# Joining an out projection and a feed-forward by halves of the tokens

## The chip, the cores and the metric

The kernel runs on one core of a Trainium2 chip. The metric is the device time of one execution in microseconds (us), the median of repeated runs. A core has five engines that each work through a list of instructions of their own, in order: TensorE (PE, the matrix engine), VectorE (DVE), ScalarE (ACT), GpSimd (POOL) and SyncE (SP, which here starts the loads). They wait for one another by semaphores.

## The reference, cut to what matters

The program computes two blocks of a transformer, one after the other, for 512 tokens of width 1024, all in fp32. The change lies in the opening block, between its mixer and its feed-forward:

```python
mixed = groups @ w_out[i]                       # out projection, 1024 x 1024
h = h + rmsnorm(mixed, ln_post_mix[i])          # first norm
f = rmsnorm(h, ln_pre_ffn[i])                   # second norm
g, up = jnp.split(f @ w_gate_up[i], 2, axis=-1) # 1024 x 5632
y = (jax.nn.silu(g) * up) @ w_down[i]           # 2816 x 1024
h = h + rmsnorm(y, ln_post_ffn[i])
```

The second block needs, among much else, a vector `mod = cond @ ada_w[i] + ada_b[i]` per layer, with `ada_w` of 1024 x 6144. This product of a single row is done on DVE, beside the matmuls of other stages.

## The kernel before, in words

Values lie with features on the 128 partitions and the 512 tokens in the free dimension. A tensor of width 1024 is eight tiles 128x512 (`X0..X7`, and `M0..M7` in buffers named `hh0..hh7`). A fp32 matmul is made of three faster ones: each operand is split into a high part, rounded to a shorter form, and a low part, the rest; `mm3` issues low weight x high value, high x high, high x low. Weights come in slabs: one load of 128x1024 (`raw`, four buffers), then in `unit` per half a cast on ACT (`whi`) and a subtraction on DVE (`wlo`), seven buffers of 512 columns each. A slab of w_gate_up is 24 matmuls and gives 128 features for all tokens; a slab of w_out is 12 here (its other half was done earlier), one of w_down 66.

A norm has several steps (`norm_cols`, `norm_rows`): squares on ACT, their sum over eight tiles on POOL or DVE (`acc`), four matmuls of one column against ones (PE, `tt<-ones1k,acc`), plus epsilon on DVE (`ms`), power -1/2 on POOL (`rc`), four small matmuls that spread the result over the partitions (`tt<-ident,rc`), a copy on DVE. The scale of the second norm is applied not to the operand but to the outputs of gate_up (`g` and `u` times `R`), so its matmuls can start before it is known.

The join goes in this order. For each of eight w_out slabs DVE multiplies the result with the scale of the attention half and adds it to M (L550, L551), ACT squares it, POOL adds the square to `macc` (DVE for the last), and ACT scales M by its column of ln_post_mix (L554, L555). Then the first norm; then `post` (L630, L631) for each of eight tiles, M x R and X + M, and `split_scaled`: ACT scales X into a high part (L275), DVE computes the low part (L276). The first four gate_up slabs run together, tile by tile of X (three `mm` banks and `po`), so that PE can begin with the first tile of X. Then come the second norm and gate_up slabs 4 to 43, one by one. A pair of slabs gives g and u of one of 22 feature tiles: DVE multiplies both with R (L733, L736), ACT applies Silu, POOL multiplies (L737), ACT and DVE split the result into `Hh` and `Hl` (L266, L267). w_down reads all 22.

From slab 4 on each slab is followed by `self.step()`, one step of the ada chain: a load of 128x1024 into the only `ada` buffer and one multiply-and-reduce on DVE (a dot, L813). The next load can start only when the dot before it is done. 40 dots belong to the first group of columns.

The order of instructions on each engine is made by a scheduler from the data flow and the order of the code; `self.order(True)` pins PE's list to the order of the code, up to `self.order(False)`. `keep_in_program_order` keeps the dots in sequence. `homes` opens two pools of memory, at the bottom and the top, and puts the tile names of a list into the lower one.

## Time and profile before

| what | value |
| --- | --- |
| three runs, median (lowest to highest) | 1908.2 us (1907.35 to 1908.96) |
| the profiled execution, and its span | 1911.36 us, 1909.7 us |
| PE busy | 1871.8 us, 98% of the span |
| DVE, ACT, POOL busy | 68%, 47%, 20% |
| chain of waits that ended last | PE 79%, DVE 5%, ACT 1% |
| single waits of PE above 1.1 us | 7.3 (start of the program), 6.2, 5.4, 3.5, 2.0, 1.7, 1.4, 1.2, 1.2 |
| mean granted clock of PE | 0.992 of full speed |

The waits of 5.4, 3.5, 1.7, 1.4 and one of the two of 1.2 us belong to the stretch that the change touches, from 205 to 250 us. In a row of a timeline stand the start and the duration in us, the engine, the line, the operation, the tiles written and read, the shape, the number of instructions put together, and in brackets how long the engine was idle before it and what ended that. Matmuls overlap, so their duration is longer than their distance from start to start.

### The profile page before, as it was taken

The page shows a single profiled execution, that of the slowest core. Times are in us where ns is not written, and L with a number is a line of the kernel's source. Part 1 is how long each engine was busy: PE and PEld are TensorE (multiplying, and loading weights), DVE is VectorE, ACT ScalarE, POOL GpSimd, SP SyncE. Part 2 cuts the span into 40 slices and gives each one's busy share as a digit, 9 for nine tenths or more (in the row PEclk, how much of TensorE's full clock was granted, in tenths as well). Part 3 has the DMA queues.
Part 4 walks back from the last instruction along what each step waited for, and adds up shares of the span by engine and source line. Part 5 has one row for each costly group of instructions (what it writes and reads, how often), then busy time and mean ns, then how long its engine had stood idle before and what let it go on. Part 6 is the DMA issues. An engine that isn't in the chain of part 4 may idle for free.

```text
span 1909.7 us, 24071 instructions
## 1 busy us (share of the span) xinstructions
PE 1871.8 (98%) x8610; PEld 1505.3 (79%) x8610; DVE 1289.6 (68%) x2354; ACT 897.2 (47%) x1664; POOL 373.4 (20%) x348
## 2 busy tenths in 40 slices
PE   8999799999999999999999999999899999999999
PEld 6887688888887887777888888887666788888887
DVE  8686876566346767885988774578977677666431
ACT  5465532323334455554644443345489755444321
POOL 3201421111000303332111110013454311111000
PEclk9999899999999999999999999999999999999999
DMA  5232155556464232322465555622222133222331
GB/s 207 89 91 78 53 186 183 184 183 187 158 214 144 98 121 81 86 67 69 133 206 194 195 173 169 208 97 100 83 67 68 31 106 115 96 96 94 97 116 44
DMA packets 70381, 236.93 MB, mean 124 GB/s; under 512 B 8085, under 2 KB 8677, under 8 KB 70262
## 3 DMA queue, kind: packets, MB, share of 16 engines
q1 hardware_dynamic: 69556, 234.47, 37.9%
...
q0 software_dynamic: 128, 0.08, 0.0%
HBM read 226.87 MB, written 2.21 MB: 120 GB/s over the span
## 4 chain that ended last, share of the span: by engine, by line
PE 79%; DVE 5%; issue 1%; ACT 1%; POOL 0%; POOLq 0%; ACTq 0%; DVEq 0%
PE mm L95 47%; PE sc L95 26%; PE po L95 3%; PE tt L98 2%; PE tt L95 1%; DVE isc L1141 1%; DVE m L1140 1%; DVE hl L899 0%; DVE v L1078 0%; DVE rst L223 0%; DVE isc L1121 0%; DVE q L897 0%; ACT A L671 0%; DVE acc L986 0%; DVE rst L224 0%
## 5 line engine op out<-in xcount | busy, mean ns | idle before, releaser
L112 ACT CAST whi<-raw 128x512 fp32r<-128x512 f32 (+1 forms) x550 | 326.7, 607 | 394.7 <-PE mm L95 232.2
L113 DVE TENSOR_TENSOR wlo<-raw,whi 128x512 fp32r<-128x512 f32 (+1 forms) x518 | 379.5, 741 | 193.8 <-ACT whi L112 191.3
L95 PE MATMUL mm<-hh,wlo 128*128 128x512 f32 (+1 forms) x984 | 399.6, 406 | 3.5 <-ACT hh L275 3.5
L95 PE MATMUL mm<-hl,whi 128*128 128x512 f32 (+1 forms) x1016 | 394.9, 392 | 0.0
L95 PE MATMUL mm<-hh,whi 128*128 128x512 f32 (+1 forms) x984 | 385.3, 392 | 0.0
L95 PEld LDWEIGHTS mm<-hl,whi 128*128 128x128 f32 (+1 forms) x1016 | 191.4, 188 | 41.3
L813 DVE CUSTOM_DVE_ANT_0 ada<-ada,bc 128x1024 f32<-128x1024 f32 x112 | 140.3, 1252 | 123.8 <-DMA ada<-in_ada_w 103.7
L95 PEld LDWEIGHTS mm<-hh,wlo 128*128 128x128 f32 (+1 forms) x984 | 185.7, 189 | 47.3 <-issue 8.5
L95 PEld LDWEIGHTS mm<-hh,whi 128*128 128x128 f32 (+1 forms) x984 | 185.8, 189 | 36.2 <-issue 1.1
L95 PE MATMUL sc<-hh,wlo 128*128 128x512 f32 x432 | 168.8, 391 | 0.0
L95 PE MATMUL sc<-hh,whi 128*128 128x512 f32 x432 | 168.4, 390 | 0.0
L95 PE MATMUL sc<-hl,whi 128*128 128x512 f32 x432 | 168.3, 390 | 0.0
L204 POOL TENSOR_TENSOR acc<-acc,sq 128x512 f32<-128x512 f32 x53 | 89.4, 1687 | 395.5 <-ACT sq L209 387.9
L1052 POOL TENSOR_TENSOR g<-g,u 128x512 f32<-128x512 f32 x44 | 63.0, 1432 | 413.0 <-DVE u L1048 358.1
L95 PE MATMUL mm<-Hh,wlo 128*128 128x512 f32 x364 | 143.3, 394 | 0.0
L95 PE MATMUL mm<-Hh,whi 128*128 128x512 f32 x364 | 143.0, 393 | 0.0
L95 PE MATMUL mm<-Hl,whi 128*128 128x512 f32 x364 | 143.0, 393 | 0.0
L266 ACT CAST Hh<-g 128x512 fp32r<-128x512 f32 x66 | 41.0, 622 | 168.4 <-POOL g L737 104.1
L95 PEld LDWEIGHTS sc<-hh,whi 128*128 128x128 f32 x432 | 81.4, 188 | 16.9
L95 PEld LDWEIGHTS sc<-hh,wlo 128*128 128x128 f32 x432 | 81.4, 188 | 16.9
L95 PEld LDWEIGHTS sc<-hl,whi 128*128 128x128 f32 x432 | 81.3, 188 | 16.9
L95 PE MATMUL sc<-Hh,wlo 128*128 128x512 f32 x220 | 86.7, 394 | 0.0
...
## 6 DMA issues: line engine op xcount, KB each, us to landing
...
```

Source lines behind the costliest of these rows:

```text
L95: self.queue(self.nc.tensor.matmul(*args, **kw))
L98: self.queue(self.nc.tensor.transpose(*args))
L112: nc.scalar.copy(hi[:, :w], raw[:, c:c + w])
L113: (eng or nc.vector).tensor_sub(lo[:, :w], raw[:, c:c + w], hi[:, :w].bitcast(F32))
L204: (eng or self.nc.gpsimd).tensor_add(acc, acc, self.square(src))
L266: self.nc.scalar.copy(hi, src)
L813: nc.vector.tensor_tensor_reduce(raw, raw, row, scale=1.0, scalar=0.0, op0=ALU.mult, op1=ALU.add, accum_out=out))
L1052: nc.gpsimd.tensor_mul(g, g, u)
L1140: nc.vector.max(m8, work[qb][:, :L])
L1141: nc.vector.match_replace(work[qb][:, :L], m8, work[qb][:, :L], SENT)
```

## The change

- Slabs 0 to 3 of w_out stay as they were; slabs 4 to 7 are done first for tokens 0 to 255 and then for tokens 256 to 511, with four banks open. All sums of squares for the first norm go to DVE. Squares of the last slab are not added but taken as a second group of column matmuls.
- The columns of the first norm for the first half come after slab 5 of the second half, its rows after slab 6 of the second half; columns of the second half after tile 1 and rows after tile 3 of the feed-forward's first half.
- The first three gate_up slabs (not four) run tile by tile, first for one half of the tokens and then for the other. Slab 3 follows whole, then the columns of the second norm, slab 4, its rows, slab 5. PE's list is pinned until there.
- The column scale of ln_post_mix is part of the first DVE operation of the new `operand`; eight multiplications on ACT go. Its result is scaled by the norm's rows where they lie, without a copy.
- The operand has its own tiles (high parts in the `hl` buffers, low parts in `Hh0..Hl3`), the first four feed-forward tiles lie in `hh` buffers, and the lower pool has `Hh0..Hh12` and `Hl0..Hl12`.
- The first ada step stands in the code behind slab 5; it stood behind slab 4.

```diff
+            def merge(n, ps, hs):
+                m = self.t(at, [P, S], F32, "sb", bufs=2)[:, hs]
+                nc.vector.tensor_mul(m, ps[:, hs], Ra[:, hs])
+                nc.vector.tensor_add(M[n][:, hs], M[n][:, hs], m)
+
+            for n in range(4):
                 if n < 3:
                     ps = pss[n]
                 else:
                     ps = self.mm_ps()
                     self.slabs([ps], [self.unit(a["w_out"][n][:, :512], (512,))], ms[:4])
-                m = self.t(at, [P, S], F32, "sb", bufs=2)
-                nc.vector.tensor_mul(m, ps, Ra)
-                nc.vector.tensor_add(M[n], M[n], m)
-                macc = self.add_square(macc, M[n], eng=nc.vector if n == 7 else None)
-                if n:
-                    nc.scalar.mul(M[n - 1], M[n - 1], self.col("ln_post_mix", n - 1))
-            nc.scalar.mul(M[7], M[7], self.col("ln_post_mix", 7))
-        _, R = self.stats(macc, self.ones1k, out="bc")
-        return X, M, R
+                merge(n, ps, slice(0, S))
+                macc = self.add_square(macc, M[n], eng=nc.vector)
+            last = [self.t(self.sp, [P, S], F32, "sq", bufs=2) for _ in range(2)]
+            pss = [self.mm_ps(), self.mm_ps(), self.sc_ps(), self.sc_ps()]
+            ws = [self.unit(a["w_out"][n][:, :512], (512,)) for n in range(4, 8)]
+            for h in range(2):
+                hs = self.half(h)
+                for n in range(4, 8):
+                    self.slabs([pss[n - 4][:, hs]], [ws[n - 4]], [(hi[:, hs], lo[:, hs]) for hi, lo in ms[:4]])
+                    merge(n, pss[n - 4], hs)
+                    sq = self.square(M[n][:, hs], last[n % 2][:, hs])
+                    if n < 7:
+                        nc.vector.tensor_add(macc[:, hs], macc[:, hs], sq)
+                    if h and n == 5:
+                        tt = self.t(self.pp, [P, 2, S], F32, "tt", bufs=1)
+                        rc = self.half_cols(tt[:, 0, :], macc, last[1], 0)
+                    if h and n == 6:
+                        R = self.half_rows(tt[:, 1, :], rc, 0)
+        return X, M, R, macc, last[1]
+
+
...
+    def half_cols(self, pc, acc, sq, h):
+        nc = self.nc
+        for tb in (2 * h, 2 * h + 1):
+            ts = slice(tb * P, (tb + 1) * P)
+            self.matmul(pc[:, tb:tb + 1], acc[:, ts], self.ones1k[:, 0:1], start=True, stop=False)
+            self.matmul(pc[:, tb:tb + 1], sq[:, ts], self.ones1k[:, 0:1], start=False, stop=True)
+        ms = self.t(self.sp, [P, NB], F32, "ms", bufs=2)[:, :2]
+        nc.vector.tensor_scalar(ms, pc[:, 2 * h:2 * h + 2], EPS, None, op0=ALU.add)
+        rc = self.t(self.sp, [P, NB], F32, "rc", bufs=3)[:, :2]
+        nc.gpsimd.tensor_tensor(rc, ms, self.mhalf[:, :2], op=ALU.pow)
+        return rc
+
+    def half_rows(self, pb, rc, h):
+        for i in range(2):
+            tb = 2 * h + i
+            self.matmul(pb[:, tb * P:(tb + 1) * P], rc[:, i:i + 1].to_broadcast([P, P]), self.ident, start=True, stop=True)
+        return pb
...
-            ps = self.four()
-            w = self.units([a["w_gate_up"][i] for i in range(4)])
+        with self.homes("ffn", [f"H{p}{i}" for p in "hl" for i in range(13)]) as fp:
+
+            xs = [(self.t(self.xp, [P, S], F32R, f"hl{k}", bufs=1), self.t(fp, [P, S], F32R, f"H{'hl'[k % 2]}{k // 2}", bufs=1))
+                  for k in range(KD)]
+
+            def operand(R, hs):
+                for k in range(KD):
+                    (hi, lo), col = xs[k], self.col("ln_pre_ffn", k)
+                    nc.vector.scalar_tensor_tensor(M[k][:, hs], M[k][:, hs], self.col("ln_post_mix", k), R[:, hs], op0=ALU.mult, op1=ALU.mult)
+                    nc.vector.tensor_add(X[k][:, hs], X[k][:, hs], M[k][:, hs])
+                    nc.scalar.activation(hi[:, hs], X[k][:, hs], AF.Copy, scale=col)
+                    nc.vector.scalar_tensor_tensor(lo[:, hs], X[k][:, hs], col, hi[:, hs].bitcast(F32), op0=ALU.mult, op1=ALU.subtract)
+                return [(hi[:, hs], lo[:, hs]) for hi, lo in xs]
+
+            ps = [self.mm_ps() for _ in range(3)]
+            w = self.units([a["w_gate_up"][i] for i in range(3)])
+            for h in range(2):
+                hs = self.half(h)
+                xh = operand(R, hs)
+                for k in range(KD):
+                    self.slabs([p[:, hs] for p in ps], w, xh, ks=[k])
+                    if h == 0 and k == 1:
+                        rc = self.half_cols(self.sc_ps(), macc, last, 1)
+                    if h == 0 and k == 3:
+                        R = self.half_rows(self.sc_ps(), rc, 1)
             for k in range(KD):
-                self.post(X, M, R, k)
-                xs.append(self.split_scaled(X[k], self.col("ln_pre_ffn", k), k))
-            self.slabs(ps, w, xs)
-            for k in range(KD):
-                acc = self.add_square(acc, X[k])
-            _, R = self.stats(acc, self.ones1k)
+                acc = self.add_square(acc, X[k], eng=nc.vector)
+
+            def slab(i, p):
+                self.slabs([p], [self.unit(a["w_gate_up"][i])], xs)
+                ps.append(p)
+
+            slab(3, self.bank("po"))
+            rc = self.norm_cols(acc, self.ones1k)
+            slab(4, self.sc_ps())
+            R = self.norm_rows(rc)
+            slab(5, self.sc_ps())
+            self.order(False)
             self.ada = (step for l in range(2) for step in self.ada_steps(l))
-            hs = []
+            self.turn, hs = 4, []
             for n in range(KF):
                 if n > 1:
                     for j in range(2):
-                        ps.append(self.any_ps())
-                        self.slabs(ps[-1:], [self.unit(a["w_gate_up"][2 * n + j])], xs)
+                        if n > 2:
+                            slab(2 * n + j, self.any_ps())
                         self.step()
...
+                if n < 4:
+                    hi, lo = (self.t(self.xp, [P, S], F32R, f"hh{2 * n + j}", bufs=1) for j in range(2))
+                    nc.scalar.copy(hi, g)
+                    nc.vector.tensor_sub(lo, g, hi.bitcast(F32))
+                    hs.append((hi, lo))
+                else:
+                    hs.append(self.split(g, n, "H", fp))
```

The lists of instructions move as follows. PE before, at the end of w_out: the last three matmuls (`mm_2204`), columns and rows of the first norm, and the first matmuls of gate_up slabs 0 to 2 (`mm_2257` to `mm_2259`).

```order
L95 MATMUL mm_2204<-hl_549_2001,wlo_2208 128x512
L95 MATMUL mm_2204<-hl_549_2001,whi_2207 128x512
L95 MATMUL mm_2204<-hl_550_2002,whi_2207 128x512
L95 MATMUL tt_2235<-ones1k_101,acc_2084 128x1 [waits DVE_49,PE_49]
L95 MATMUL tt_2235<-ones1k_101,acc_2084 128x1 x3
L95 MATMUL tt_2244<-ident_96,rc_2242 128x128 [waits Pool_49]
L95 MATMUL tt_2244<-ident_96,rc_2242 128x128 x3
L95 MATMUL mm_2257<-hh_634_2303,wlo_2270 128x512 [waits Activation_49]
L95 MATMUL mm_2257<-hh_634_2303,whi_2269 128x512
L95 MATMUL mm_2258<-hh_634_2303,wlo_2274 128x512
L95 MATMUL mm_2258<-hh_634_2303,whi_2273 128x512
L95 MATMUL mm_2259<-hh_634_2303,wlo_2278 128x512
```
PE after, around the rows of half 0 (`tt_605<-ident`), between the halves of w_out slab 6 (`sc_585`) and slab 7 (`sc_586`):

```order
L95 MATMUL sc_585_2127<-hl6_549_2001,wlo_595_2144 128x256
L95 MATMUL sc_585_2127<-hl6_549_2001,whi_594_2143 128x256
L95 MATMUL sc_585_2127<-hl7_550_2002,whi_594_2143 128x256
L95 MATMUL tt_605_2254<-ident_11_96,rc_607_2261 128x128 [waits Pool_49]
L95 MATMUL tt_605_2254<-ident_11_96,rc_607_2261 128x128
L95 MATMUL sc_586_2128<-mh0_373_1463,wlo_598_2150 128x256
L95 MATMUL sc_586_2128<-mh0_373_1463,whi_597_2149 128x256
L95 MATMUL sc_586_2128<-ml0_374_1464,whi_597_2149 128x256
```
and at the end of slab 7, with the first matmuls of gate_up slabs 0 and 1 (`mm_626`, `mm_627`):

```order
L95 MATMUL sc_586_2128<-hl6_549_2001,wlo_598_2150 128x256
L95 MATMUL sc_586_2128<-hl6_549_2001,whi_597_2149 128x256
L95 MATMUL sc_586_2128<-hl7_550_2002,whi_597_2149 128x256
L95 MATMUL mm_626_2324<-hl0_610_2308,wlo_633_2334 128x256 [waits Activation_49]
L95 MATMUL mm_626_2324<-hl0_610_2308,whi_632_2333 128x256
L95 MATMUL mm_626_2324<-Hh0_611_2309,whi_632_2333 128x256 [waits DMASW3_49,DVE_49,PE_49]
L95 MATMUL mm_627_2325<-hl0_610_2308,wlo_635_2338 128x256
L95 MATMUL mm_627_2325<-hl0_610_2308,whi_634_2337 128x256
```
Columns and rows of the first norm moved ahead of the last w_out matmuls, and the feed-forward follows these directly.

DVE after, at the same place: `sb_609` is the merge of slab 7, half 1, the `hh` tiles are M, `Hh0_611` a low part of the operand.

```order
L542 TENSOR_TENSOR sb_609_2294<-sc_586_2128,sacc_563_2055 128x256 [waits PE_49]
L754 SCALAR_TENSOR_TENSOR hh0_438_1647<-hh0_438_1647,consts_9_89,tt_605_2254 128x256
L563 TENSOR_TENSOR acc_570_2084<-acc_570_2084,sq_581_2123 128x256 [waits Activation_49]
L543 TENSOR_TENSOR hh7_547_1990<-hh7_547_1990,sb_609_2294 128x256 [waits DVE_49]
L755 TENSOR_TENSOR X0_1_81<-X0_1_81,hh0_438_1647 128x256 [waits DVE_49]
L754 SCALAR_TENSOR_TENSOR hh1_462_1721<-hh1_462_1721,consts_9_89,tt_605_2254 128x256
L754 SCALAR_TENSOR_TENSOR hh2_481_1775<-hh2_481_1775,consts_9_89,tt_605_2254 128x256
L757 SCALAR_TENSOR_TENSOR Hh0_611_2309<-X0_1_81,consts_9_89,hl0_610_2308 128x256 [waits DMASW3_49,Activation_49]
```
The first scaling of the operand (L754) stands behind the merge (L542); before, the copy of the norm's rows and L630 stood here.

DVE before, at the first dots (L813): `ms` and `R` belong to the second norm, `g` and `u` to feed-forward tiles 0 and 1.

```order
L813 ISA ada_2541,mod_17_111<-ada_2541,bc_2539 128x1024 [waits DMAHW1_49]
L813 ISA mod_17_111 128x1
L241 TENSOR_SCALAR ms_2473<-tt_2468 128x4 [waits PE_49]
L113 TENSOR_TENSOR wlo_2595<-raw_2592,whi_2594 128x512 [waits DMAHW0_49,Activation_49]
L113 TENSOR_TENSOR wlo_2599<-raw_2592,whi_2598 128x512 [waits Activation_49]
L113 TENSOR_TENSOR wlo_2633<-raw_2630,whi_2632 128x512 [waits DMAHW2_49,Activation_49]
L258 COPY R_2482<-tt_2477 128x512 [waits PE_49]
L733 TENSOR_TENSOR g_2484<-mm_2257,R_2482 128x512 [waits DMASW3_49,DVE_49]
L736 TENSOR_TENSOR u_2487<-mm_2258,R_2482 128x512
L733 TENSOR_TENSOR g_2494<-mm_2259,R_2482 128x512
L736 TENSOR_TENSOR u_2497<-po_2260,R_2482 128x512
L813 ISA ada_2579,mod_17_111<-ada_2579,bc_2539 128x1024 [waits DMAHW7_49]
```
DVE after, at the first dot (L881):

```order
L258 COPY R_2684<-tt_2679 128x512 [waits PE_49]
L795 TENSOR_TENSOR g_2721<-mm_2324,R_2684 128x512 [waits DVE_49]
L798 TENSOR_TENSOR u_2724<-mm_2325,R_2684 128x512
L795 TENSOR_TENSOR g_2731<-mm_2326,R_2684 128x512
L798 TENSOR_TENSOR u_2734<-po_2600,R_2684 128x512
L113 TENSOR_TENSOR wlo_2852<-raw_2845,whi_2851 128x512 [waits Activation_49]
L803 TENSOR_TENSOR hh_682_2728<-g_2721,hh_681_2727 128x512 [waits Activation_49]
L803 TENSOR_TENSOR hh_686_2738<-g_2731,hh_685_2737 128x512 [waits Activation_49]
L881 ISA ada_2743,mod_17_111<-ada_2743,bc_2741 128x1024 [waits DMAHW5_49]
```
The first dot moved from ahead of the second norm to behind it, its four multiplications and two splits.

DVE before, at dot 40 (`ada_1027`) and the u of the last feed-forward tile (`u_1029`):

```order
L813 ISA ada_1027_4213,mod0_17_111<-ada_1027_4213,bc_677_2539 128x1024 [waits DMAHW3_49,DVE_49]
L813 ISA mod0_17_111 128x1
L824 TENSOR_TENSOR mod0_17_111<-mod0_17_111,consts_9_89 128x40 [waits DVE_49]
L831 SCALAR_TENSOR_TENSOR A0_19_113<-mod0_17_111,consts_9_89 128x8 [waits DVE_49]
L831 SCALAR_TENSOR_TENSOR A1_20_114<-mod0_17_111,consts_9_89 128x8
L736 TENSOR_TENSOR u_1029_4218<-mm_1021_4177,R_662_2482 128x512 [waits PE_49]
```
and after (`ada_1031`, `u_1033`):

```order
L881 ISA ada_1031_4380,mod0_17_111<-ada_1031_4380,bc_687_2741 128x1024 [waits DMAHW5_49,DVE_49]
L881 ISA mod0_17_111 128x1
L798 TENSOR_TENSOR u_1033_4385<-mm_1025_4344,R_672_2684 128x512 [waits PE_49]
L815 TENSOR_TENSOR u_1038_4395<-sq_1036_4392,g_1037_4394 128x512
L892 TENSOR_TENSOR mod0_17_111<-mod0_17_111,consts_9_89 128x40 [waits DVE_49]
```
In both lists the last u stands behind the last dot; the three small operations that stood between them moved behind it.

## Rows read from the trace of the kernel before

**Rows 1.** Timeline of PE at the join: start, duration, line, tiles, idle before.

```profile
194.85 0.39 PE L95 MATMUL mm<-mh,wlo 128*128 128x512 f32 x1
...
211.25 1.84 PE L95 MATMUL tt<-ones1k,acc 128*128 128x1 f32 x8 [5.36 <-DVE acc L204]
214.44 2.08 PE L95 MATMUL tt<-ident,rc 128*128 128x128 f32 x8 [1.35 <-POOL rc L243]
219.99 0.80 PE L95 MATMUL mm<-hh,wlo 128*128 128x512 f32 x1 [3.47 <-ACT hh L275]
...
245.36 0.95 PE L95 MATMUL tt<-ones1k,acc 128*128 128x1 f32 x8
248.04 1.98 PE L95 MATMUL tt<-ident,rc 128*128 128x128 f32 x8 [1.74 <-POOL rc L243]
249.68 0.77 PE L95 MATMUL sc<-hh,wlo 128*128 128x512 f32 x1
...
267.00 0.39 PE L95 MATMUL sc<-hh,wlo 128*128 128x512 f32 x1
```

**Rows 2.** Timeline of PE: two matmuls of 512 columns, 36 apart.

```profile
454.69 0.39 PE L95 MATMUL sc<-hh,wlo 128*128 128x512 f32 x1
...
462.85 0.39 PE L95 MATMUL mm<-hh,wlo 128*128 128x512 f32 x1
```

**Rows 3.** Timeline of DVE: dots 1, 7, 37, 38, 39 and 40 of the first forty.

```profile
244.78 1.22 DVE L813 CUSTOM_DVE_ANT_0 ada<-ada,bc 128x1024 f32<-128x1024 f32 x1
...
280.98 1.23 DVE L813 CUSTOM_DVE_ANT_0 ada<-ada,bc 128x1024 f32<-128x1024 f32 x1 [2.21 <-DMA ada<-in_ada_w]
...
450.05 1.22 DVE L813 CUSTOM_DVE_ANT_0 ada<-ada,bc 128x1024 f32<-128x1024 f32 x1
...
456.07 1.23 DVE L813 CUSTOM_DVE_ANT_0 ada<-ada,bc 128x1024 f32<-128x1024 f32 x1 [2.23 <-DMA ada<-in_ada_w]
...
461.55 1.22 DVE L813 CUSTOM_DVE_ANT_0 ada<-ada,bc 128x1024 f32<-128x1024 f32 x1
...
471.61 1.22 DVE L813 CUSTOM_DVE_ANT_0 ada<-ada,bc 128x1024 f32<-128x1024 f32 x1
```

**Rows 4.** Timeline of PE: two matmuls of 256 columns between longer ones.

```profile
158.16 0.40 PE L95 MATMUL sc<-k,qs 128*128 128x256 f32 x2
158.40 0.39 PE L95 MATMUL mm<-mh,wlo 128*128 128x512 f32 x1
```

**Rows 5.** Timeline of DVE and POOL at the two norms of the join.

```profile
213.13 0.16 DVE L241 TENSOR_SCALAR ms<-tt 128x4 f32<-128x4 f32 x1 [2.02 <-PE tt L95]
213.37 1.02 POOL L243 TENSOR_TENSOR rc<-ms,mhalf 128x4 f32<-128x4 f32 x1 [4.93 <-DVE ms L241]
...
220.30 1.41 DVE L276 SCALAR_TENSOR_TENSOR hl<-X,consts,hh 128x512 fp32r<-128x512 f32 x2
...
250.06 0.69 DVE L258 COPY R<-tt 128x512 f32<-128x512 f32 x1 [1.74 <-PE tt L95]
...
257.14 0.68 DVE L267 TENSOR_TENSOR Hl<-g,Hh 128x512 fp32r<-128x512 f32 x1
```

**Rows 6.** Groups by line and shape: count, busy us, mean ns, idle before.

```profile
L95 PEld LDWEIGHTS sc<-k,qs 128*128 128x128 f32 x192 | 36.0, 188 | 8.1
...
L113 DVE TENSOR_TENSOR wlo<-raw,whi 128x256 fp32r<-128x256 f32 x24 | 10.2, 424 | 23.2 <-ACT whi L112 23.2
...
L1268 ACT ACTIVATE sb<-Th,ri 128x256 f32<-128x256 f32 x16 | 8.0, 503 | 0.2
```

**Rows 7.** Timeline of PE: a wait of two microseconds later in the program.

```profile
1298.92 0.41 PE L98 MATMUL tt<-ident,Th 8*128 8x8 f32 x4 [2.02 <-ACT Th L1101]
```

**Rows 8.** Windows: busy time of PE, PEld, DVE, ACT, POOL, then granted clock.

```profile
1300.00:1305.00 5.00, 5.00 (x17) 3.92 (x17) 1.19 (x2) 1.83 (x4) 0.72 (x1) 0.71 0.50 157
```

**Rows 9.** Timeline of ACT and PE: the last feed-forward tile made, and first used.

```profile
475.73 0.62 ACT L266 CAST Hh<-g 128x512 fp32r<-128x512 f32 x1 [3.98 <-POOL g L737]
...
482.84 0.39 PE L95 MATMUL mm<-Hh,wlo 128*128 128x512 f32 x1
```

More of the change, by code (lines that the diff above doesn't have):

```diff
@@ L532, in mixer_a @@
             aacc = aacc[0]
+            self.order(True)
             pss = []
@@ L542, in mixer_a @@
                     Ra = self.norm_rows(rc, self.t(mp, [P, S], F32, "sacc", bufs=1))
-            for n in range(8):
+            def merge(n, ps, hs):
[3 more added lines that the diff above has]
+            for n in range(4):
                 if n < 3:
@@ new lines, in mixer_a, with half @@
+        return X, M, R, macc, last[1]
+    def half(self, h):
+        return slice(h * S // 2, (h + 1) * S // 2)
+    def half_cols(self, pc, acc, sq, h):
[9 more added lines that the diff above has]
+        return rc
@@ L706, in av, with ffn_a @@
         return out, tr, mul
-    def ffn_a(self, X, M, R):
+    def ffn_a(self, X, M, R, macc, last):
         tc, nc, a = self.tc, self.nc, self.a
         acc, xs = None, []
-        with self.homes("ffn", [f"Hh{i}" for i in range(KF)] + [f"Hl{i}" for i in range(8, 12)]) as fp:
-            ps = self.four()
-            w = self.units([a["w_gate_up"][i] for i in range(4)])
-            for k in range(KD):
-                self.post(X, M, R, k)
-                xs.append(self.split_scaled(X[k], self.col("ln_pre_ffn", k), k))
-            self.slabs(ps, w, xs)
-            for k in range(KD):
-                acc = self.add_square(acc, X[k])
-            _, R = self.stats(acc, self.ones1k)
+        with self.homes("ffn", [f"H{p}{i}" for p in "hl" for i in range(13)]) as fp:
[20 more added lines that the diff above has]
+                        R = self.half_rows(self.sc_ps(), rc, 1)
+            for k in range(KD):
+                acc = self.add_square(acc, X[k], eng=nc.vector)
[8 more added lines that the diff above has]
+            self.order(False)
@@ L752, in ffn_a @@
                 macc = self.add_square(macc, ps, eng=nc.vector if n == 7 else None)
-                M.append(self.t(self.xp, [P, S], F32, f"hh{n}", bufs=1))
+                M.append(self.t(self.xp, [P, S], F32, f"hl{n}", bufs=1))
                 nc.scalar.mul(M[n], ps, self.col("ln_post_ffn", n))
@@ L764, in ffn_a @@
                 self.slabs([ps], [[(hi[:, c:], lo[:, c:])]], es)
-                e = self.t(fp, [P, S], F32, f"Hh{n}", bufs=1)
+                e = self.t(fp, [P, S], F32, f"Hh{14 + n}", bufs=1)
                 nc.scalar.copy(e, ps)
@@ L772, in ffn_a @@
                 self.post(X, M, R, k)
-                xs.append(self.split(X[k], 8 + k, "H", fp))
+                xs.append(self.split(X[k], k, "H", fp))
             if self.stop == 2:
@@ L1026, in ffn_conv @@
         tc, nc, a = self.tc, self.nc, self.a
-        with self.homes("ffn", [f"Hh{i}" for i in range(KF)] + [f"Hl{i}" for i in range(8, 12)]) as fp:
+        with self.homes("ffn", [f"H{p}{i}" for p in "hl" for i in range(13)]) as fp:
             w = a["ffn_w_up"][l]
```

6 lines of the change are left out of this document (1 added, 5 removed).

## The prediction

> **What bounds the kernel now.** I read the page first: the matrix engine (PE) is busy for 98% of the span, so time can only be won where PE waits, where its clock is down, or where its matmuls are cheaper. The waits of PE come next: of the seven longest single ones, four lie within 40 us (the table under the profile before has them), between the last out-projection slabs and the first feed-forward slabs. The timeline of PE for that stretch is [rows 1]. From the first matmul of w_out slab 4 (194.85) to the first of gate_up slab 7 (267.00, counted from 0) it takes 72.15 us. The work in it: 4 slabs of 12 matmuls and 7 of 24, 216 matmuls. A matmul of 512 columns takes 0.227 us from start to start (36 of them in 462.85 - 454.69 = 8.16 us [rows 2]), so 49.0 us, and four small groups for the two norms, 0.95 us each at full clock [rows 1]: 3.8 us. That is 52.8 us of work and 19.3 us of loss. Four waits make 11.9 us of it: 5.36 for the sum of squares of the whole slab 7, 1.35 for the power on POOL, 3.47 for the first scaled operand, 1.74 for the second power. Most of the rest is the clock: the matmuls at 219.99 and 249.68 last 0.80 and 0.77 us, where later ones last 0.39.
>
> After this stretch PE runs slab after slab without a wait. Beside it runs a second chain: 40 dots of the ada vector, one 128x1024 multiply-reduce on DVE each, on a single buffer. Dot 7 starts at 280.98, dot 39 at 461.55 [rows 3]: 32 steps of 5.64 us, while a gate_up slab takes 24 x 0.227 = 5.44. So this chain is slower than PE, and it stands in DVE's order between the weight splits that PE needs. It is harmless in the kernel before only because it starts early: dot 1 stands ahead of the second norm, at 244.78, 22.2 us before slab 7.
>
> **The change, part by part.**
>
> *Matmuls.* Slabs 4 to 7 of w_out become 96 matmuls of 256 columns, and three (not four) gate_up slabs 144 of them; slabs 3 to 6 of gate_up stay whole, 96 of 512. The trace has no long run of 256-column matmuls. The nearest row is a pair between long ones, 0.24 us for two [rows 4], 0.12 each; half of a long one is 0.1134. I take 0.117: 240 x 0.117 = 28.1, and 96 x 0.227 = 21.8. The norms become two halves of the first (about 1.4 us each: four 1-column sums against acc and the last square, two row matmuls) and one whole, 1.9: 4.7 us. Work after: 54.6 us, 1.8 more than before. Bounds of the pitch, 0.1134 to 0.12: -0.9 to +0.7 us; what a weight load could do to it is a rival below.
>
> *Waits that go.* Sums of squares and power of the first half of the tokens lie now beside slabs 6 and 7 of the second half; the 5.36 us and the 3.47 us lose their cause, and one of the two powers gets cover. What is late next, in the order of the rows shown:
> (a) Rows of half 0 stand behind only slab 6's half, 12 x 0.117 = 1.4 us. From ms to the row matmul it took 214.44 - 213.13 = 1.31 to 1.7 us [rows 1, 5]. With the way from PE to DVE, 0.5 us are left.
> (b) The first feed-forward operand. The first scaling STT stands on DVE behind the merge of slab 7, half 1, which waits for PE's last w_out matmul. Then: merge 0.42, STT of 256 columns 0.45, three adds at 0.34 to the next, ACT with scale 0.50, and four hand-overs of about 0.07 (213.29 to 213.37 is one). The 256-column prices come from [rows 6] (424 and 503 ns), the STT is worked out as half of 0.70 plus its start [rows 5]. Sum 2.7 us of PE waiting.
> (c) Rows of half 1. Their ms stands behind 14 STT and 9 adds of the operand of half 0: 14 x 0.38 + 9 x 0.335 = 8.3 us after the 0.5 of the merge, then 0.16 + 1.3 + 0.1 for the power: 10.4 us after the last w_out matmul. PE gets there after 2.7 + 36 x 0.117 + 0.9 for the columns = 7.8. Wait 2.6 us.
> (d) The power of the whole norm now has slab 4 (5.44 us) as cover, more than the 1.7 it needs: 0. For small misses 0.3.
> Sum 6.1 us. The clock: behind a wait of 2.02 us [rows 7] the next window of 5 us shows a mean granted clock of 0.71 [rows 8], so matmuls ran there at 1.2 GHz for a part of it, and 5 x 0.29 = 1.5 us were lost. The same should follow (b); but what is lost there eats into the wait (c), whose end is set by DVE. I add 0.5. Bounds for waits and clock together: 4 us (no drop, DVE a fifth faster) to 11 (each drop paid in full, DVE a fifth slower).
>
> Stretch after: 54.6 + 6.1 + 0.5 = 61.2 against 72.15: **the join gains 11 us** (bounds 6 to 14).
>
> *Adds from POOL to DVE, 8 column scalings of ACT folded into the STT.* DVE has room beside w_out; what its order costs is in (b) and (c). Where the homes of tiles lie (13 low tiles, the operands in other buffers) adds no instruction in PE's path: 0, covered by PE's work; if a tile came free later than used, PE would show a wait at the first Hh tile.
>
> *The dots move.* In the changed order dot 1 stands behind the copy of the second norm, four multiplies and two splits. In the trace before, the second of these splits ended at 257.14 + 0.68, 7.8 us after the copy at 250.06 [rows 5]. The copy is at about the start of slab 5 + 0.4, so slab 7 is 10.5 us after it and dot 1 stands 2.7 us before slab 7, not 22.2: 19.5 us later against PE. Part comes back: before, dots 1 to 40 took 471.61 - 244.78 = 226.8 us, with gaps early, and 10 us before the last; without gaps 39 x 5.64 = 220.1. Left: 12.8 us. What depends on dot 40: the u multiply of the last gate_up pair stands behind it on DVE in both orders, then POOL's product, then ACT's Hh21, which the first down slab needs. Before, Hh21 was done at 476.35 and PE used it at 482.84 [rows 9]: 6.5 us of slack, and 0.4 more, since three small operations that stood between the dot and u now stand behind it. 12.8 - 6.9 = **5.9 us given back**, at the end of the first w_down slab (a part perhaps a few us earlier, at the weight splits behind dot 39). The clock falls once more behind such a wait, 1.5 as above. Bounds: with every step at 5.48 (456.07 to 461.55 [rows 3]) nothing of it is left; with each pair 5.48 + 6.02 (450.05 to 456.07) it is 39 x 0.11 = 4.3 more, 10.2.
>
> Sum: -11.0 + 5.9 + 1.5 = -3.6 us. Against the profiled execution's 1911.4 us that is 1907.8; the three timed runs have their median at 1908.2, 3.2 below the profiled one, so the forecast is **1904.6 us**.
>
> **Rivals.**
> - *The dots cost nothing* (a step of 5.48, or the lead of the weight splits is enough). For it: every second step is about 5.48. Against: the others wait for their transfer, 2.2 us at a time [rows 3], and 5.64 is a mean over 32 steps. The time: 1908.2 - 11 = 1897.2.
> - *The dots or the two waits take all.* Dots at 5.75 give 4.3 us more of stall, or (b) and (c) are 3 to 4 us longer: 1908.2 - 3.6 + 4 = 1908.6, no change.
> - *Slower: a weight load for each half.* Each 256-column matmul has a load of its own, 188 ns by its row [rows 6], and 120 more are issued. If a load can't run beside the matmul ahead of it, or only partly, loads set the pitch: 240 x (0.188 - 0.117) = 17 us more, 1908.2 - 3.6 + 17 = 1921.6. It decides from a pitch of 0.132 on (3.6/240 above 0.117). Against it: the pair of [rows 4] ran at 0.12 with loads of 188 ns. For it: a pair may live on loads done ahead, under long matmuls; a run of 144 can't. The Trainium skill ("TensorE: Matmul & The Clock Gate", Part 3) speaks for this rival: it says a weight load overlaps matmuls in flight only when its row group differs, and all of these use all rows. By that rule even 512-column matmuls would show their loads, and the pitch of 0.227 in [rows 2], with 188 ns loads, says they don't.
>
> **How the numbers follow.** The forecast, the join's gain with about half of it given back: 0.42, own range 1901 to 1907.5. Dots free: 0.20 (1897). All taken: 0.26 (1906 to 1911). Weight loads, or that halves otherwise don't do what they should: 0.12 (1911 to 1922). The range of eight in ten takes in the first three with the join's bounds: 1896.5 to 1912. About 0.2% (3.8 us) is what this kernel's measurement tells from no change; the forecast lies at that bound, so it is shared: faster 0.21 + 0.20 + 0.04 = 0.45; same 0.21 + 0.18 = 0.39; slower 0.04 + 0.12 = 0.16.
>
> **What would show it.** The stretch from w_out slab 4 to gate_up slab 7 near 61 us; PE waits of some 2.7 us for the first operand (ACT) and 1 to 3 us for POOL's rc, none above 3.5; 256-column matmuls at 0.117 from start to start. Dot 1 some 3 us before slab 7, dots 5.64 apart, and a PE wait of 4 to 6 us for Hh21 (or DVE's wlo) in the first w_down slab, with a lower granted clock behind it. I am wrong if no such wait is there, if dots run nearer than 5.5 us, or if the halves run at 0.15 or more.

## The result, and the profile after

The changed kernel takes 1898.2 us (median of 4 runs, 1896.15 to 1899.15) against 1908.6, a ratio of 0.9936 with a 95% interval of 0.9924 to 0.9947. On two other chips it was 1894.4 and 1894.1 (0.9926 and 0.9930). So it is faster by 10 to 14 us. The forecast was a gain of 3.6: the measured time lies in the stated range, near the rival's 1897.2 ("the dots cost nothing"), but the gain is about three times the forecast.

The profiled execution took 1897.3 us, its span is 1895.6. The page, busy time by engine:

```profile
PE 1866.1 (98%) x8738; PEld 1510.1 (80%) x8738; DVE 1290.5 (68%) x2401; ACT 894.3 (47%) x1668; POOL 349.3 (18%) x336
```

PE's share is the same (98 or 99% in every run here); the time went out of waits, of stretches at a low clock and of the pitch of matmuls (the time from one start to the next), which a busy share does not show. Three of the waits of PE, in us in total, times, longest:

```profile
...
PE mm L95 <- ACT hl L756: 2.7, 1, 2.7
...
PE tt L95 <- DVE acc L204: 1.2, 1, 1.2
...
PE sc L95 <- ACT Hh L266: 1.0, 1, 1.0
```

Only the first lies in the join. The timeline of PE at the join, to be held against [rows 1]:

```profile
194.19 0.28 PE L95 MATMUL mm<-mh,wlo 128*128 128x256 f32 x1
...
195.62 0.28 PE L95 MATMUL mm<-mh,wlo 128*128 128x256 f32 x1
...
197.06 0.28 PE L95 MATMUL sc<-mh,wlo 128*128 128x256 f32 x1
...
209.89 0.39 PE L95 MATMUL mm<-hl,wlo 128*128 128x256 f32 x1 [2.73 <-ACT hl L756]
...
218.94 0.60 PE L95 MATMUL sc<-ident,rc 128*128 128x128 f32 x4
...
255.95 0.39 PE L95 MATMUL mm<-hl,wlo 128*128 128x512 f32 x1
```

Windows of 5 us there (busy time of PE, PEld, DVE, ACT and POOL, then the granted clock):

```profile
210.00:215.00 5.00, 4.78 (x26) 4.39 (x26) 5.00 (x15) 2.24 (x5) 0.00 (x0) 0.68 0.03 11
215.00:220.00 5.00, 5.00 (x30) 5.00 (x31) 3.67 (x11) 1.11 (x3) 0.87 (x1) 0.63 0.00 0
220.00:225.00 5.00, 5.00 (x44) 5.00 (x43) 5.00 (x15) 3.69 (x8) 0.00 (x0) 1.00 0.02 3
```

*The join* came out near the sum that was worked out. From w_out slab 4 to gate_up slab 7 it takes 255.95 - 194.19 = 61.8 us, forecast 61.2, before 72.15: 10.4 us gained. The first operand comes 2.73 us late, forecast 2.7. Halves run at 0.12 us from start to start at full clock (12 of them from 195.62 to 197.06), forecast 0.117. The wait (a) of 0.5 and the wait (c) of 2.6 us did not come; in their place the clock stayed down longer (0.68 and 0.63 in two windows, which is 5 x 0.32 + 5 x 0.37 = 3.4 us lost, forecast 0.5 beside the wait). As the prediction said, slow matmuls and the wait for POOL cover each other: in a later run of the same kernel (e13 below) the clock is back one window earlier, and there PE waits 0.61 us for these rows.

*The dots.* Timeline of DVE, to be held against [rows 3] (L881 are dots 1, 34 to 36 and 38 to 40, L267 the low part of a feed-forward tile):

```profile
251.99 1.21 DVE L881 CUSTOM_DVE_ANT_0 ada<-ada,bc 128x1024 f32<-128x1024 f32 x1
...
437.06 0.69 DVE L267 TENSOR_TENSOR Hl<-g,Hh 128x512 fp32r<-128x512 f32 x1 [1.84 <-ACT Hh L266]
...
438.48 1.23 DVE L881 CUSTOM_DVE_ANT_0 ada<-ada,bc 128x1024 f32<-128x1024 f32 x1
...
444.69 1.23 DVE L881 CUSTOM_DVE_ANT_0 ada<-ada,bc 128x1024 f32<-128x1024 f32 x1 [2.42 <-DMA ada<-in_ada_w]
...
448.96 0.69 DVE L267 TENSOR_TENSOR Hl<-g,Hh 128x512 fp32r<-128x512 f32 x1 [1.84 <-ACT Hh L266]
449.57 1.22 DVE L881 CUSTOM_DVE_ANT_0 ada<-ada,bc 128x1024 f32<-128x1024 f32 x1
...
459.02 1.23 DVE L881 CUSTOM_DVE_ANT_0 ada<-ada,bc 128x1024 f32<-128x1024 f32 x1 [1.89 <-DMA ada<-in_ada_w]
...
463.60 1.23 DVE L881 CUSTOM_DVE_ANT_0 ada<-ada,bc 128x1024 f32<-128x1024 f32 x1 [1.54 <-DMA ada<-in_ada_w]
...
468.46 1.23 DVE L881 CUSTOM_DVE_ANT_0 ada<-ada,bc 128x1024 f32<-128x1024 f32 x1 [2.69 <-DMA ada<-in_ada_w]
```

Dot 1 stands 255.95 - 251.99 = 4.0 us before slab 7 (forecast 2.7). To dot 35 the steps are as long as before: 444.69 - 251.99 = 192.7 us for 34, 5.67 each (forecast 5.64). But the last five are 4.5 to 4.9, 23.8 us and not 28.2; the same five lie between 4.5 and 4.9 in e6, e9, e10, e11 and e13 below. Two things go with the shorter steps. Dot 36 has only Hl ahead of it (448.96), where dot 34 has Hl (437.06) and a weight split ahead of it. And the transfers are quicker: from the end of a dot to the next, which waits for its load, it is 444.69 - 439.71 = 5.0 us for dot 35, but 463.60 - 460.25 = 3.4 for dot 39. SP's queue shows a difference (loads of `raw`, L107, and of `ada`, L878):

```profile
438.38 0.33 SPq L107 DMA_DIRECT2D raw<-in_w_down  x1
439.74 0.33 SPq L878 DMA_DIRECT2D ada<-in_ada_w  x1
...
460.28 0.33 SPq L878 DMA_DIRECT2D ada<-in_ada_w  x1
461.48 0.33 SPq L107 DMA_DIRECT2D raw<-in_w_down  x1
```

A weight load was started 1.4 us ahead of the longer transfer, and behind the shorter one. So it is along the whole list: the loads of dots 5, 7 and on to 35 start 1.1 to 1.4 us behind a weight load and land 4.2 to 4.8 us after their start, those of dots 37 and 39, with no weight load so near ahead, land after 3.1 to 3.2. That the weight load is the cause was not tried.

The balance is then 5.9 - 1.3 (dot 1 earlier) + 0.9 (34 steps at 5.67) - 4.4 (the last five) = 1.1 us, and PE waited 1.0 us for Hh21 (1.3 with the slow matmuls behind it), not 5.9, and no fall of the clock followed there. A second wait came up where none was forecast, at the end of w_down, where the last sum of squares stands behind a dot (before, the same wait was 0.35 us). Behind it the clock is low for 6.8 us, before for 3.4:

```profile
472.74 0.50 PE L95 MATMUL sc<-Hh,wlo 128*128 128x512 f32 x1 [0.99 <-ACT Hh L266]
...
582.50 1.05 PE L95 MATMUL tt<-ones1k,acc 128*128 128x1 f32 x8 [1.22 <-DVE acc L204]
```

*The matmuls of w_down* run faster, in all three feed-forwards. First and last matmul of the last w_down (528 matmuls), before and after:

```profile
1783.44 0.39 PE L95 MATMUL mm<-Hh,wlo 128*128 128x512 f32 x1
...
1905.27 0.40 PE L95 MATMUL sc<-Hl,whi 128*128 128x512 f32 x1
```

```profile
1770.80 0.39 PE L95 MATMUL sc<-Hh,wlo 128*128 128x512 f32 x1
...
1779.64 0.40 PE L95 MATMUL sc<-Hh,wlo 128*128 128x512 f32 x1
...
1785.83 0.40 PE L95 MATMUL mm<-Hh,wlo 128*128 128x512 f32 x1
...
1891.21 0.40 PE L95 MATMUL mm<-Hl,whi 128*128 128x512 f32 x1
```

121.83 us became 120.41, 1.4 less; the first slab after shows where: tiles 0 to 12 take 8.84 us for 39 matmuls, 0.2267 each, tiles 13 to 21 take 6.19 us for 27, 0.2293. Three such stages make 4.3 us. The prediction priced this part of the change at nothing.

The two profiled executions lie 1911.4 - 1897.3 = 14.1 us apart, the medians 10.4. Part of that is chance: 1.5 us is a lower clock far from the change, in the window of [rows 8], which the profile after does not have.

### The profile page after: what moved, and what is told of

The parts are those of the page before. It is cut to its first block, busy times and chain, and to the rows that moved or that the text cites. A ratio compares the mean times of both kernels' runs of the same rounds, so it can differ in the third digit from the quotient of the medians.

```text
span 1895.6 us, 24366 instructions
## 1 busy us (share of the span) xinstructions
PE 1866.1 (98%) x8738; PEld 1510.1 (80%) x8738; DVE 1290.5 (68%) x2401; ACT 894.3 (47%) x1668; POOL 349.3 (18%) x336
## 4 chain that ended last, share of the span: by engine, by line
PE 80%; DVE 8%; DMA 5%; issue 3%; POOL 2%; ACT 2%; POOLq 0%; SPq 0%; DVEq 0%; ACTq 0%
PE mm L95 47%; PE sc L95 24%; DMA ada<-in_ada_w 5%; PE po L95 5%; PE tt L98 2%; POOL g L799 2%; PE tt L95 2%; DVE ada L881 1%; DVE isc L1209 1%; DVE m L1208 1%; DVE u L798 1%; ACT Hh L266 1%; DVE Hl L267 0%; DVE wlo L113 0%; DVE hl L967 0%
## 5 line engine op out<-in xcount | busy, mean ns | idle before, releaser
L112 ACT CAST whi<-raw 128x512 fp32r<-128x512 f32 (+2 forms) x552 | 327.4, 607 | 381.1 <-PE mm L95 219.3
L113 DVE TENSOR_TENSOR wlo<-raw,whi 128x512 fp32r<-128x512 f32 (+2 forms) x520 | 382.5, 744 | 181.9 <-ACT whi L112 179.5
L95 PE MATMUL mm<-hl,whi 128*128 128x512 f32 (+2 forms) x1040 | 397.5, 385 | 0.0
L95 PE MATMUL mm<-hh,whi 128*128 128x512 f32 x800 | 310.0, 391 | 0.0
L881 DVE CUSTOM_DVE_ANT_0 ada<-ada,bc 128x1024 f32<-128x1024 f32 x112 | 139.3, 1244 | 134.9 <-DMA ada<-in_ada_w 108.4
L95 PE MATMUL mm<-Hl,whi 128*128 128x512 f32 (+1 forms) x468 | 180.9, 387 | 0.1
L95 PE MATMUL mm<-Hh,whi 128*128 128x512 f32 (+1 forms) x468 | 180.0, 385 | 0.2 <-issue 0.2
L95 PEld LDWEIGHTS mm<-hh,whi 128*128 128x128 f32 x800 | 150.6, 188 | 29.0 <-issue 1.1
L95 PE MATMUL sc<-hl,whi 128*128 128x512 f32 (+1 forms) x448 | 171.1, 385 | 0.0
L95 PE MATMUL sc<-Hl,whi 128*128 128x512 f32 x268 | 104.7, 391 | 0.0
L95 PE MATMUL sc<-Hh,whi 128*128 128x512 f32 x268 | 104.3, 389 | 0.0
```

The costliest lines, as they stand in the source:

```text
L95: self.queue(self.nc.tensor.matmul(*args, **kw))
L112: nc.scalar.copy(hi[:, :w], raw[:, c:c + w])
L113: (eng or nc.vector).tensor_sub(lo[:, :w], raw[:, c:c + w], hi[:, :w].bitcast(F32))
L881: nc.vector.tensor_tensor_reduce(raw, raw, row, scale=1.0, scalar=0.0, op0=ALU.mult, op1=ALU.add, accum_out=out))
```

## The experiments

Twelve runs followed, two of them of the changed kernel again. "Stretch" is the time from w_out slab 4 to gate_up slab 7 in the profile, "tail" that of the last w_down from first to last matmul start.

| kernel | median us | ratio to before (95%) | stretch | tail |
| --- | --- | --- | --- | --- |
| before | 1908.2 to 1908.8 | 1 | 72.2 | 121.8 |
| changed, first | 1898.2 | 0.9936 (0.9924 to 0.9947) | 61.8 | 120.4 |
| e9 changed | 1894.4 | 0.9926 (0.9912 to 0.9939) | 61.7 | 120.4 |
| e13 changed | 1894.1 | 0.9930 (0.9919 to 0.9942) | 60.4 | 120.4 |
| e1 list of tiles alone | 1904.6 | 0.9981 (0.9971 to 0.9991) | 72.2 | 120.4 |
| e2 changed, old list | 1902.3 | 0.9964 (0.9951 to 0.9977) | 60.7 | 121.8 |
| e3 dots early | 1893.4 | 0.9914 (0.9900 to 0.9927) | 60.4 | 120.4 |
| e5 half dots | 1893.7 | 0.9916 (0.9902 to 0.9930) | 61.5 | 120.4 |
| e6 adds on POOL | 1900.4 | 0.9951 (0.9939 to 0.9964) | 65.9 | 120.4 |
| e7 feed-forward whole | 1898.7 | 0.9945 (0.9933 to 0.9958) | 64.8 | 120.4 |
| e8 w_out whole | 1898.1 | 0.9947 (0.9934 to 0.9959) | 63.6 | 120.4 |
| e10 rotated list | 1893.3 | 0.9926 (0.9913 to 0.9939) | 60.4 | 120.5 |
| e11 long dots | 1895.2 | 0.9933 (0.9920 to 0.9946) | 60.4 | 120.4 |
| e12 early scaling | 1896.4 | 0.9941 (0.9929 to 0.9953) | 64.3 | 120.4 |

e1, e2, e3 and e5 ran together, then e6 to e9, then e10 to e13; the median of before was 1908.8, 1908.4 and 1908.3 us.

### The changed kernel again: e9, e13

Without an edit, e9 beside e6 to e8 and e13 beside e10 to e12:

> The changed kernel itself, once more beside the others of this call, so that they are compared with it on one chip. Expected: ratio to the kernel before 0.9936 to 0.9945, some 1897 to 1899 us.

> The changed kernel once more, for the comparison with the other three of this call: ratio to the kernel before 0.992 to 0.994.

Both repeat the gain (0.9926 and 0.9930); e9 lies below the 1897 to 1899 us that I had expected. Both profiles lack the wait for Hh21, and that for the last sum is 0.3 us or less.

### Where the tiles lie: e1, e2, e10

```diff
 # e1: the kernel before, in both feed-forwards
-        with self.homes("ffn", [f"Hh{i}" for i in range(KF)] + [f"Hl{i}" for i in range(8, 12)]) as fp:
+        with self.homes("ffn", [f"H{p}{i}" for p in "hl" for i in range(13)]) as fp:
 # e2: the changed kernel with the line of before; e10: in ffn_conv alone, range(9, 22) for range(13)
```

> The kernel before with one part of the change alone: the list of tiles for the lower pool is Hh0..Hh12 and Hl0..Hl12 in both feed-forwards. Theory (place): matmuls of w_down run at a mean pitch of 0.2312 us in the kernel before and 0.2284 in the changed one, and this comes from where the tiles lie; so here the pitch of the three w_down stages (528 matmuls each) falls to about 0.228, each stage gets 1.2 to 1.5 us shorter, and the program 2.5 to 4 us faster, ratio 0.998 to 0.9987. Rival (the prediction's): where tiles lie costs nothing, pitch 0.2312 and ratio 1.000.

> The changed kernel with the old list of tiles for the lower pool (Hh0..Hh21, Hl8..Hl11). Theory (place): the join stays at 61.8 us and the w_down stages go back to a pitch of about 0.231; 2.5 to 4 us of the gain of 10.4 to 12 us are lost, ratio to before 0.9955 to 0.9965. Rival (place costs nothing): as the changed kernel, 0.9936.

> The changed kernel; in the two later feed-forwards the lower pool holds the whole tiles 9 to 21 (Hh9..Hh21, Hl9..Hl21) instead of 0 to 12. Theory (address): in their w_down the matmuls on tiles 9 to 21 run at 0.2267 us save the first few, those on tiles 0 to 8 at a mean of 0.229; the stage stays at 120.0 us (121.4 with the old list), and so does the program. Rival (order in the slab: the first tiles of a slab are the fast ones): tiles 0 to 12 stay at 0.2267 and the last nine at 0.229.

e1 alone is 4.2 us faster than before, with the join unchanged. Its eleven runs lie in two groups, six from 1903.0 to 1904.6 us and five from 1907.3 to 1908.9, so the median says little by itself (the interval of the ratio allows 1.7 to 5.5 us); the profile says more, where the last w_down is again 120.4 us:

```profile
1777.30 0.39 PE L95 MATMUL mm<-Hh,wlo 128*128 128x512 f32 x1
...
1897.71 0.40 PE L95 MATMUL sc<-Hl,whi 128*128 128x512 f32 x1
```

e2 goes back to 121.8. Its ratio lies in the expected range, but against e9 and e13 it loses 7 to 8 us, more than the three w_down stages hold: its gate_up slabs read four low parts of the operand (Hl0 to Hl3) from the upper pool, and from slab 7 to the first w_down it takes 206.2 us where every other kernel takes 201.3. In e10 the fast tiles moved with the list. A slab (tiles 0 to 21), with the last nine tiles of the one before it:

```profile
1780.00 0.39 PE L95 MATMUL sc<-Hh,wlo 128*128 128x512 f32 x1
...
1786.12 0.40 PE L95 MATMUL mm<-Hh,wlo 128*128 128x512 f32 x1
...
1792.32 0.40 PE L95 MATMUL mm<-Hh,wlo 128*128 128x512 f32 x1
```

Tiles 13 to 21 now take 6.12 us for 27 matmuls (0.2267) and tiles 0 to 8 6.20 (0.2296). So it is the place and not the order in the slab, and the prediction's zero fell.

### The dots: e3, e5, e11

```diff
 # e3: the first two steps behind slabs 3 and 4, before the second norm; the two behind slab 5 go
+            self.ada = (step for l in range(2) for step in self.ada_steps(l))
             slab(3, self.bank("po"))
+            self.step()
             rc = self.norm_cols(acc, self.ones1k)
             slab(4, self.sc_ps())
+            self.step()
...
 # e5: half of each load and dot
-            nc.sync.dma_start(raw, src)
+            nc.sync.dma_start(raw[:, :512], src[:, :512])
...
 # e11: in front of dots 11 to 14
+                self.tc.keep_in_program_order(nc.vector.tensor_tensor(raw, raw, raw, op=ALU.max))
```

> The changed kernel with the first two steps of the ada chain put behind gate_up slabs 3 and 4 in the code, ahead of the second norm; still 40 steps. Theory (chain): the whole chain of dots starts some 8 us earlier, dot 40 comes earlier by some us, PE's wait of 1.0 us for Hh21 at the end of the first w_down slab goes, and the program is 1 to 1.5 us faster than the changed kernel. Rival 1: the dot in front of the second norm delays ms or R on DVE, PE waits longer at the rows of the second norm, and nothing is won or 1 us lost. Rival 2 (prediction's 5.64 us per step held to the end): the wait before would have been 5.9 us, and the gain here 5 us or more.

> The changed kernel with each ada step cut to half: 128x512 are loaded and multiplied instead of 128x1024, so the second half of every sum is left out. Theory (chain): steps get shorter than 5 us where they waited for their transfer and stay near 4.9 to 5.5 where the chain u, POOL, ACT, Hl sets them; PE's waits for Hh21 (1.0 us) and, at the end of the last w_down slab, for the acc behind a dot (1.2, in the kernel before 0.35) fall to 0.4 or less; 1.5 to 3 us faster than the changed kernel. Rival: these waits have another cause and stay, gain under 0.5 us.

> The changed kernel with four of the 40 steps of the ada chain made longer: a maximum of the tile with itself, 128x1024 on DVE (about 1.2 us, the values stay), before the dots 11 to 14. Theory (the chain ends just when PE needs it, with a slack of about 0 to 1 us in the changed kernel): dot 40 comes 4 to 5 us later, and PE waits 3 to 6 us more for Hh21 or a wlo in the first w_down slab; 3 to 6 us slower than the changed kernel. Rival 1 (slack of 5 us or more, the waits there had other causes): no new wait, no slower than 1 us. Rival 2 (the prediction: 5.9 us of wait already there): the same 5 us more, but from a wait of 6 to one of 11.

In e3 and e5 both waits are gone (Hh21; acc 0.2 us or less). From the first matmul of the first w_down to the first of the projection behind the feed-forward's last norm it takes 140.5 us in the first profile of the changed kernel, 137.1 in e3 and 135.2 in e5, where the clock does not fall at that norm. But it is 137.1 in e9 and 136.8 in e13 too, which have neither wait. In the timed runs they are at 0.9914 and 0.9916, the changed kernel at 0.9926 to 0.9936: a gain of 2 to 4 us, with intervals that overlap, and not the 5 or more of rival 2. So what the dots take, with the clock behind the waits, is 0 to 3.4 us in the profiles and differs from run to run.

My expectation for e11 was wrong, and what rival 1 forecast came. Four maxima of 1.2 us were added to the first chain (and, by the same condition, four to a later one, at 974 to 994 us), and no new wait came up: the medians of e11 and e13 are 1.0 us apart, within the intervals. Timeline of DVE behind the last of them, dots 14 to 16:

```profile
329.82 1.22 DVE L883 CUSTOM_DVE_ANT_0 ada<-ada,bc 128x1024 f32<-128x1024 f32 x1
...
334.41 1.23 DVE L883 CUSTOM_DVE_ANT_0 ada<-ada,bc 128x1024 f32<-128x1024 f32 x1 [1.55 <-DMA ada<-in_ada_w]
...
335.56 0.69 DVE L267 TENSOR_TENSOR Hl<-g,Hh 128x512 fp32r<-128x512 f32 x1
...
339.07 1.23 DVE L883 CUSTOM_DVE_ANT_0 ada<-ada,bc 128x1024 f32<-128x1024 f32 x1 [1.02 <-DMA ada<-in_ada_w]
```

The steps behind the four longer ones (6.2 to 7.2 us) are 4.6 to 4.8 us, five of them, and make much of the delay good. Here, as in the last four steps of the changed kernel, no wait for Hh stands ahead of the dot, only its transfer. Where Hl stands ahead with a weight split behind it (437.06 above), DVE first waits 1.84 us in line for POOL's product and ACT's Hh: those are the steps of 5.48 and more. e11 is not a clean test, since the added operations also changed the order of the list; it shows that 5.64 is no length of the chain's own.

### The parts of the join: e6, e7, e8, e12

```diff
 # e6
-                macc = self.add_square(macc, M[n], eng=nc.vector)
+                macc = self.add_square(macc, M[n])
...
 # (and the adds of the halves and of X)
 # e7: columns and rows of half 1 at once; the operand of both halves; then
...
+            for k in range(KD):
+                self.slabs(ps, w, xs, ks=[k])
 # e8: w_out slabs 4 to 7
+                self.slabs([pss[n - 4]], [ws[n - 4]], ms[:4])
...
 # e12: e3, and in mixer_a, behind the rows of half 0, ahead of slab 7's merge; rows of half 1 at k == 5
+                        for k in range(2):
+                            self.scaled(X, M, R, k, self.half(0))
...
```

> The changed kernel with the additions of squares (w_out slabs 0 to 7, and the eight of the second norm) back on POOL. Theory: DVE ran adds of 0.69 us in 1.77 while POOL worked in the kernel before, and the last add before the first columns is on the way to them; PE's waits in the join (2.7 for the first operand, 0 for the rows of half 0) grow by 1 to 3 us, the stretch from w_out slab 4 to gate_up slab 7 becomes 63 to 65 us instead of 61.8. Rival: DVE, with 16 adds less, gets to the operand sooner than POOL disturbs it, and the stretch is the same or up to 1 us shorter.

> The changed kernel with the halves undone in the feed-forward: the second half of the first norm follows w_out at once, the operand is made for both halves tile by tile, and gate_up slabs 0 to 2 run whole. Theory (overlap): PE has nothing to do from the last w_out matmul through the columns, power and rows of half 1 (about 0.9 + 1.7 + 0.5) and the first operand (about 3), 5 to 6 us of waits instead of 2.7 + 0.2, with the clock down behind them; 144 halves less give back 0.9. Stretch 64.5 to 67 us, 3 to 5 us slower than the changed kernel. Rival (the gain was in w_out's halves and the adds): the stretch stays within 1 us of 61.8.

> The changed kernel with the halves undone in w_out: slabs 4 to 7 whole, columns and rows of half 0 behind slab 7, the feed-forward by halves as in the changed kernel. Theory (overlap): PE waits for the last square and add as in the kernel before (4.5 to 5.5 us), for the power (1.3) and for the first operand (2 to 2.7), 8 to 9 us of waits instead of 2.9, so the stretch is 66 to 69 us, 5 to 7 us slower than the changed kernel. Rival (the gain was in the feed-forward's halves): within 2 us of 61.8.

> The kernel with early dots (e3), and the scaling of tiles 0 and 1 of the first half (STT and add on DVE) ahead of the merge of w_out slab 7, half 1; the rows of the second half of the first norm behind tile 5 instead of 3. Theory: PE's wait of 2.73 us for the first operand was DVE's list (merge, scaling, three adds, then ACT); it falls to 0.5 to 1.5 us, the clock does not fall behind it or later, and the stretch from w_out slab 4 to gate_up slab 7 goes from 60.4 to 61.8 us to 57.5 to 59.5; 2 to 4 us faster than the changed kernel with the early dots counted in. Rival: DVE's 18 us for the two halves of the operand set the end, the wait only moves to later tiles, and the stretch stays at 60 to 62 us.

e6 is 6.0 us slower than the changed kernel beside it, the most of the three. Its wait for the first operand is 1.12 us and not 2.73, but four others stand behind it (0.64, 0.83, 0.88 and 1.97), the last two in the second half of the tokens, whose operand DVE now brings late. DVE is slower while POOL adds, as the expectation said: two additions to X take 2.93 us beside POOL here, 0.75 in e9. PE, then POOL and DVE of e6, then DVE of e9:

```profile
231.07 0.39 PE L95 MATMUL mm<-hl,wlo 128*128 128x256 f32 x1 [0.88 <-ACT hl L756]
...
233.54 0.39 PE L95 MATMUL mm<-Hh,whi 128*128 128x256 f32 x1 [1.97 <-DVE Hh L757]
```

```profile
227.35 4.26 POOL L204 TENSOR_TENSOR acc<-acc,sq 128x512 f32<-128x512 f32 x3 [1.90 <-ACT sq L209]
...
228.96 2.93 DVE L755 TENSOR_TENSOR X<-X,hh 128x256 f32<-128x256 f32 x2
```

```profile
227.65 0.75 DVE L755 TENSOR_TENSOR X<-X,hh 128x256 f32<-128x256 f32 x2
```

The clock falls twice (0.66 in the windows from 210 and from 235 us), and the stretch is 4.2 us longer than in e9. e7 (PE) has the waits that it should have, 4.5 us in three large ones (expected 5 to 6), and is 4.3 us slower:

```profile
209.53 0.38 PE L95 MATMUL sc<-ones1k,acc 128*128 128x1 f32 x2 [1.48 <-DVE acc L563]
...
212.42 1.23 PE L95 MATMUL sc<-ident,rc 128*128 128x128 f32 x4 [1.21 <-POOL rc L584]
215.49 0.80 PE L95 MATMUL mm<-hl,wlo 128*128 128x512 f32 x1 [1.85 <-ACT hl L756]
```

e8 is 3.7 us slower, less than the 5 to 7 expected: its waits are 5.8 us instead of 8 to 9. The sum of squares comes sooner here (0.81 and 2.08 us of wait, against 5.36 in [rows 1]); its additions are on DVE instead of POOL and the last square is not added at all, and which of the two does it was not tried:

```profile
207.87 0.35 PE L95 MATMUL tt<-ones1k,acc 128*128 128x1 f32 x2 [0.81 <-DVE acc L562]
210.30 0.38 PE L95 MATMUL tt<-ones1k,sq 128*128 128x1 f32 x2 [2.08 <-ACT sq L209]
...
212.15 1.18 PE L95 MATMUL tt<-ident,rc 128*128 128x128 f32 x4 [1.02 <-POOL rc L581]
215.18 0.58 PE L95 MATMUL mm<-hl,wlo 128*128 128x256 f32 x1 [1.84 <-ACT hl L753]
```

So each part carries 4 to 6 us of the program's time while the others are there. Not all of it lies in the join: the stretch is some 4 (e6), 3 (e7) and 2 us (e8) longer than in e9, and the profiles of these three also show waits at the dots that e9's does not have (1.06 us for the last sum in e6, 1.03 for Hh21 in e7, 1.58 for the last sum in e8), of the kind that comes and goes between runs. All five runs of e6 and of e8 are slower than every run of e9, of e7 four of five; the intervals of e7 and e8 overlap a little with that of e9. No kernel took back two parts at once.

e12 was meant to beat the changed kernel and did not (1896.4 against 1894.1). The wait for the first operand fell to 1.43 us, but the first low part now stands in DVE's list behind the merge, a weight split and one more scaling, from 211.40 to 211.88 us, and PE waits 2.00 us until then (the view names no releaser):

```profile
209.48 0.39 PE L95 MATMUL mm<-hl,wlo 128*128 128x256 f32 x1 [1.43 <-DVE acc L563]
...
211.98 0.55 PE L95 MATMUL mm<-Hh,whi 128*128 128x256 f32 x1 [2.00 <-issue]
```

That is 3.4 us of waits instead of 2.9, and the clock is down in three windows:

```profile
210.00:215.00 5.00, 3.02 (x14) 3.06 (x15) 5.00 (x14) 2.14 (x5) 0.00 (x0) 0.63 0.30 105
215.00:220.00 5.00, 5.00 (x25) 5.00 (x25) 4.28 (x12) 1.49 (x4) 1.07 (x1) 0.50 0.00 0
220.00:225.00 5.00, 5.00 (x38) 5.00 (x38) 0.94 (x3) 0.00 (x0) 0.00 (x0) 0.85 0.01 3
```

Its theory fell; the rival (the wait moves) held, at 64.3 us more strongly than it said, though a part of that is the clock of this one profile. By its ratio to before e3 is the fastest kernel measured; that it beats the changed kernel is not shown, the intervals overlap.

## Why the prediction was wrong

- *The join* (11 us) was right: 10.4 in the first profile, 11.8 in that of e13. The sum of waits and clock was right (7.2 us beside the 54.6 of work, forecast 6.6), their split was not, so that the closeness of the sum is in part luck.
- *The dots* (5.9 us and 1.5 for the clock) is the step that failed. It took a mean step of 5.64 us, measured in the middle of the order before, for all 39 steps of the new one. The first 34 took 5.67. At the end of the list Hl and the weight loads stand otherwise: the next dot starts 3.3 to 3.7 us after the end of the one before, in four cases of five behind nothing but its transfer, and I did not look at that end of the order. The steps to dots 36 to 40 took 4.5 to 4.9 us, 4.4 us less in all, and dot 1 came 1.3 us earlier than forecast. So the wait for Hh21 was 1.0 us or none, and the dots cost 0 to 3.4 us with all that followed, not 7.4. Nor is the step a property of the chain: e11 made four of them longer, and those behind them shortened to 4.6. The bound below ("nothing of it is left") and its rival at 0.20 held the truth; the choice between the bounds was wrong. By its own signs (a wait of 4 to 6 us, no dots nearer than 5.5) the prediction is refuted in this part.
- *The homes of tiles*, priced at 0 "since no instruction is added", cost 4.3 us of pitch before the change: 1.4 in each of three stages, and e1 and e2 show it from both sides. This term had no reason but that no instruction was added. The trace of before had it: 0.2267 in gate_up [rows 2] and 121.83 / 527 = 0.2312 in w_down, one and the same instruction. I had taken the pitch from one stage and not compared the other.
- *Slower by weight loads* did not happen: at full clock the halves ran at 0.12 us one behind the other, each with a load that lasts 188 ns by its row [rows 6]. The rule of the Trainium skill ("TensorE: Matmul & The Clock Gate", Part 3), that a load overlaps matmuls in flight only with another row group, is not what this trace shows.
- The two errors are 7.4 - (0 to 3.4) and 4.3 us, together 8 to 12, and make up the difference of 7 to 11 us between the forecast gain and the measured ones. That the first result (1898.2) lies by the rival's 1897.2 is luck: the rival priced the tiles at nothing too, and the first profile does show waits at the dots.
